# Two-part start of a hybrid diffusion layer: 768 token columns through two projection blocks, then the last 512

## The chip, the cores and the metric

The kernel runs on one core of a Trainium2 chip. The metric is device time in microseconds of one execution of the whole program; lower is better. All names of engines are those of the profile: PE (TensorE matmul), PEld (TensorE weight load), DVE (VectorE), ACT (ScalarE), POOL (GpSimd), SP (SyncE, which issues most DMAs).

## The reference

One layer over 256 context tokens and 1024 latent tokens, model width 1024, everything in float32. What matters here is its beginning:

```python
def rms_norm(x, w):
    y = xf * lax.rsqrt(jnp.mean(xf * xf, axis=-1, keepdims=True) + EPS)
    return y * w
def modulate(h, shift, scale):
    return h * (1 + scale) + shift
```

`shift` and `scale` come from SiLU(c) for latent tokens and SiLU(c_ctx) for context tokens through one linear map `w_ada` (adaLN). So the normed and modulated input is h = x * root * w1s + shift, with one root factor per token (column) and one w1s = (1 + scale) * norm weight and one shift per channel (row), different for context and latent. One input projection of h follows: gated DeltaNet q, k, v, z and gates, and neighbourhood attention q, k, v. Then come short convolutions, two scans, attention, the output projection with a gated residual, and a SwiGLU feed-forward.

## The kernel before, in words

Tokens lie in the free dimension: `xcT[k]` is 128 channels by 1280 tokens (`CT` = 256 context columns first, then 1024 latent), for k = 0..7 (`KT` = 8). `SEGS` cuts the 1280 columns into 256, 512 and 512, one PSUM bank each. PSUM has 8 banks, which `bank(name)` hands out.

Float32 products are made of three products in the faster fp32r form: each operand is split into a high part and a rounding remainder (`hh[k]`, `hl[k]` for h; `whi`, `wlo` for a weight block), and PE adds hi*hi, hi*lo and lo*hi. The remainder needs the high part first: `hh` is written on ACT, `hl` is h minus `hh`.

The beginning, with the lines of the profile:

- SP issues, in this order, the eight x tiles of 1280 columns (L686), two raw weight blocks (`fraw`, L690), `w_ada` tiles 0 to 2 (L682, 1 MB each), constants `cst` and `masks` (L693, L694), `w_ada` tiles 3 to 7, and small tables.
- Squares on ACT (L743, L745), pairs added on DVE (L746), summed over channels by a product with ones on PE (L748, in plain float32, which PE makes in two passes), Ln and Exp on ACT (L750, L751): the root factors `rs`, in SBUF.
- The weight blocks of the first two jobs, `first[0]` and `first[1]` (keys of head 0 and 1), are split on DVE and on POOL (L201, L204).
- `ada(j)` multiplies SiLU(c) with w_ada tile j on PE (L712) and copies the row to SBUF (L714). `column(j)` turns that row into columns on PE (L720) and writes `mod1` (shift) and `w1s` on DVE (L722, L725). `keep_busy` issues products whose result nobody reads (L759).
- `normed_tile(k)`: for each stretch of columns x * w1s * rs on DVE (L732), then hh = that + shift on ACT (L733); then hl = (that + shift) - hh on DVE (L735).
- For k = 0 the products of both blocks are written out by hand (L773); for k = 1..7 `normed_tile(k+1)` is issued ahead of `b.mm([k])` for both blocks (L419: nine products of 256, 512, 512 columns), and `AHEAD` says behind which of them the next `ada` and `column` stand.

In this part (`tc.manual_schedule`) PE, DVE and ACT run in the order in which the code is written. Outside it a planner orders instructions by its own estimates.

Behind the part, each block is evacuated (`evac`: a scaled copy on ACT at L452, four taps of the convolution on DVE at L461, reading the bank in PSUM), and the next jobs follow: `jobs[2]` is another key block, whose weights are split at L203 and L204 and whose high part takes the place of block 0's. Its products need three banks: two are free, one comes from block 0's evacuation.

Of the kernel before, what the change touches and what calls it, by code (L numbers as in the profile page):

```python
# [9 lines left out]
F32 = mybir.dt.float32  # L10
# [4 lines left out]
OP = mybir.AluOpType  # L15
# [5 lines left out]
KT = 8  # L21
# [67 lines left out]
def hybrid(ctx, tc, a, dbg):  # L89
# [83 lines left out]
    act.activation(sc2, c2, AF.Silu)  # L173
# [215 lines left out]
    with ExitStack() as bs:  # L389
# [281 lines left out]
        first = [Block("k", 0), Block("k", 1)]  # L671
        with ExitStack() as xs:
            xp = pools(xs, "xp", "left")
            xt = []
            masks = xp.tile([128, 4, 128], F32, name="masks", tag="masks")
            ascope = ExitStack()
            wap = pools(ascope, "wap", "right", 7)
            aw = {}

            def load_ada(j):  # L680
                aw[j] = w = wap.tile([128, KT, 256], F32, name="wada", tag="wada")
                sp.dma_start(w, a["wa1"][j])  # L682

            for k in range(KT):
                x = xp.tile([128, T], F32, name=f"xt{k}", tag=f"xt{k}")
                sp.dma_start(x, a["xcT"][k])  # L686
                xt.append(x)
            raws = [xp.tile([128, KT, 128], F32, name=f"fraw{i}", tag=f"fraw{i}") for i in range(2)]
# [15 lines left out]
            rs = xp.tile([128, T], F32, name="rs", tag="rs")  # L704
            rows = {}

            def ada(j, copy):
# [6 lines left out]
                copy(rows[j], p[:, :256])  # L714

            def column(j):

                p, row = bank("pm"), rows.pop(j)
                for b in range(2):
                    pe.matmul(p[:, 2 * b:2 * b + 2], row[:, b * 128:(b + 1) * 128], sel, start=True, stop=True)  # L720
                m = mod1.rearrange("p (s b) c -> p s b c", s=2)[:, :, j]
                dve.tensor_tensor(m, p[:, 0:4].rearrange("p (s c) -> p s c", s=2),  # L722
                                  bada[:, 0:16].rearrange("p (s b) -> p s b", s=2)[:, :, j:j + 1].to_broadcast(
                                      [128, 2, 2]), OP.add)
                dve.tensor_scalar(w1s[:, j], m[:, 1], 1.0, n1w[:, j:j + 1], op0=OP.add, op1=OP.mult)  # L725

            def normed_tile(k, cuts=(slice(0, CT), slice(CT, T))):
                t = xt[k]
                parts = [(x, mod1[:, k, int(x.start < CT):int(x.start < CT) + 1]) for x in cuts]
                for x, sh in parts:  # L730
# [7 lines left out]
            with tc.manual_schedule(engines={mybir.EngineType.PE, mybir.EngineType.DVE, mybir.EngineType.Activation}):  # L738
# [29 lines left out]
                for b in first:  # L768
                    b.banks()
# [1071 lines left out]
```

## Time and profile before

| What | Value |
|---|---|
| time, median of 3 runs | 1489.84 us (1489.16 to 1491.1) |
| profiled execution, its time | 1489.21 us |
| its span, first to last instruction | 1487.5 us |
| PE busy | 1451.1 us, 98% of the span |
| DVE, ACT, POOL busy | 995.0, 703.9, 106.7 us |
| mean granted TensorE clock | 0.999 |
| first product of a projection block | 25.43 us |
| first product of the third block | 65.31 us |

How to read a row. In the timeline: start in us, busy us, engine, line, operation, output<-inputs, shape, count of merged instructions, and in brackets the idle time before it and what ended it. In the groups: line, engine, operation, names and shapes, count, then busy us and the mean ns of one, then the idle time of the engine before them. Matmuls are pipelined: the pitch from one start to the next says more than the busy time of one.

### The profile page before, as it was taken

What the parts mean: (1) busy time and instruction counts of PE and PEld (TensorE: products, weight loads), DVE (VectorE), ACT (ScalarE), POOL (GpSimd) and SP (SyncE); (2) the same over time, 40 slices, a digit from 0 to 9 for tenths busy, and PEclk for the clock granted to TensorE, in tenths of its full rate; (3) what the DMA queues carried; (4) which work ended last, traced back from release to release, by engine and by line L of the source; (5) the groups of instructions that cost most, each with busy time, mean ns of one, the idle gap of its engine ahead of it and who ended that gap; (6) DMA issues with size and microseconds to landing.
All of it is one profiled execution on the core that took longest, in us unless ns stands there. A gap on an engine that the chain in (4) does not pass through costs nothing.

```text
span 1487.5 us, 23901 instructions
## 1 busy us (share of the span) xinstructions
PE 1451.1 (98%) x8708; PEld 1219.0 (82%) x8708; DVE 995.0 (67%) x1794; ACT 703.9 (47%) x1388; POOL 106.7 (7%) x208
## 2 busy tenths in 40 slices
PE   6999999999999988999999999999999999999998
PEld 4889898887898877887878888888888888888887
DVE  5783598966653546688966589665555557698652
ACT  5452544556653256667752474333333335355440
POOL 1033000311110001112100000000000000000000
PEclk9999999999999999999999999999999999999999
DMA  9265232987664488998458105333333335888742
GB/s 390 74 214 157 75 86 69 287 245 227 199 202 161 124 286 268 284 282 255 138 183 298 43 15 199 121 106 106 107 106 106 107 100 191 291 325 290 255 135 85
DMA packets 205397, 267.35 MB, mean 180 GB/s; under 512 B 15968, under 2 KB 113760, under 8 KB 204256
## 3 DMA queue, kind: packets, MB, share of 16 engines
q1 hardware_dynamic: 197680, 260.01, 54.2%
q10 hardware_dynamic: 7600, 5.81, 1.2%
q8 instruction: 69, 1.13, 0.3%
q14 instruction: 48, 0.39, 0.1%
HBM read 201.02 MB, written 68.94 MB: 181 GB/s over the span
## 4 chain that ended last, share of the span: by engine, by line
PE 59%; DMA 3%; DVE 2%; ACT 2%; issue 1%; SPq 0%; DVEq 0%; ACTq 0%
PE ps L1415 29%; PE ps L1758 14%; PE ps L1544 3%; PE sc L332 2%; PE sc L322 2%; PE ps L1392 2%; PE sc L309 1%; PE blk L615 1%; PE ps L1566 1%; PE ps L1278 1%; DMA bt<-rpb 1%; DVE bt L313 1%; PE ps L1295 1%; PE ps L1269 1%; PE ps L1259 1%
## 5 line engine op out<-in xcount | busy, mean ns | idle before, releaser
L1476 ACT CAST uhi<-wq 128x512 fp32r<-128x512 f32 x101 | 61.3, 622 | 136.5 <-issue 84.6
L1476 ACT CAST uhi<-ws 128x512 fp32r<-128x512 f32 x91 | 53.9, 621 | 147.7 <-PE ps L1415 93.3
L419 PE MATMUL blk<-hh,whi 128*128 128x512 f32 (+1 forms) x410 | 119.8, 386 | 0.5 <-ACT kk L568 0.5
L419 PE MATMUL blk<-hl,whi 128*128 128x512 f32 (+1 forms) x410 | 113.9, 370 | 0.3 <-DVE hl L735 0.3
L615 PE MATMUL blk<-zw,hh 128*128 128x256 f32 (+1 forms) x576 | 112.5, 289 | 1.0 <-ACT cr L467 1.0
L419 PE MATMUL blk<-hh,wlo 128*128 128x512 f32 (+1 forms) x410 | 112.6, 369 | 0.0
L1477 DVE TENSOR_TENSOR ulo<-wq,uhi 128x512 fp32r<-128x512 f32 x101 | 67.9, 689 | 60.2 <-ACT uhi L1476 33.8
L1415 PE MATMUL ps<-hT,uhi 128*128 128x512 f32 x336 | 103.7, 390 | 0.0
L1415 PE MATMUL ps<-hT,ulo 128*128 128x512 f32 x336 | 103.4, 389 | 0.0
L1415 PE MATMUL ps<-lT,uhi 128*128 128x512 f32 x336 | 103.4, 389 | 0.0
L615 PEld LDWEIGHTS blk<-zw,hh 128*128 128x128 f32 x576 | 90.9, 189 | 4.1 <-ACT cr L467 1.4
L1415 PE MATMUL ps<-hB,uhi 128*128 128x512 f32 x288 | 89.1, 390 | 0.0
L1415 PE MATMUL ps<-lB,uhi 128*128 128x512 f32 x288 | 88.7, 389 | 0.0
L1415 PE MATMUL ps<-hB,ulo 128*128 128x512 f32 x288 | 88.7, 389 | 0.0
L419 PEld LDWEIGHTS blk<-hl,whi 128*128 128x128 f32 x410 | 70.9, 188 | 14.1 <-DVE hl L735 0.8
L419 PEld LDWEIGHTS blk<-hh,wlo 128*128 128x128 f32 x410 | 71.1, 188 | 13.7
L615 PE MATMUL blk<-zw,hl 128*128 128x256 f32 (+1 forms) x288 | 81.8, 284 | 0.0
L419 PEld LDWEIGHTS blk<-hh,whi 128*128 128x128 f32 x410 | 67.3, 189 | 15.4 <-issue 4.0
L1415 PEld LDWEIGHTS ps<-lT,uhi 128*128 128x128 f32 x336 | 63.1, 188 | 13.1
L1415 PEld LDWEIGHTS ps<-hT,ulo 128*128 128x128 f32 x336 | 63.1, 188 | 13.1
L1415 PEld LDWEIGHTS ps<-hT,uhi 128*128 128x128 f32 x336 | 62.9, 188 | 13.0
L313 DVE CUSTOM_DVE_ANT_0 bt<-sc,bt 128x640 f32<-128x640 f32 x64 | 52.4, 821 | 29.9 <-DMA bt<-rpb 10.0
(361 smaller groups left out, 3361.5 us busy)
## 6 DMA issues: line engine op xcount, KB each, us to landing
wq<-w_fo SPq DMA_DIRECT2D x99, 256.0 KB, 4.1
wq<-w_gu SPq DMA_DIRECT2D x88, 256.0 KB, 2.9
wad<-wa SPq DMA_DIRECT2D x64, 256.0 KB, 4.3
bt<-rpb SPq DMA_DIRECT2D x64, 192.0 KB, 4.0
t_d<-g SPq DMA_DIRECT2D x22, 512.0 KB, 3.5
fr<-t_d SPq DMA_DIRECT2D x44, 256.0 KB, 4.7
f_d<-g SPq DMA_DIRECT2D x33, 256.0 KB, 2.1
fr<-f_d SPq DMA_DIRECT2D x33, 256.0 KB, 4.1
```

Source lines behind the costliest of these rows:

```text
L309: s = pe.matmul(sc[:, u * 640 + n0:u * 640 + n1], q, ks[i], start=i == 0, stop=i == 1)
L313: dve.tensor_tensor_reduce(bt, sc[:, u * 640:u * 640 + 640], bt, -1.0, 3.0e38, OP.add, OP.min, m[:, 0:1])
L322: pe.transpose(sc[:, u * 640 + j * 128:u * 640 + (j + 1) * 128], bt[:, j * 128:(j + 1) * 128], ident)
L332: return pe.matmul(sc[u * ND:u * ND + ND, 1280:1408], vv, pts[u][:, j * 128:(j + 1) * 128], start=j == 0, stop=j == 4)
L419: pe.matmul(o, ww[:, k], xx[k][:, s], start=k == 0 and j == 0, stop=k == KT - 1 and j == 2)
L615: pe.matmul(p[:, :c1 - c0], x[k][:, s], ww[:, k, c0:c1], start=k == 0 and j == 0, stop=k == KT - 1 and j == 2)
L1392: pe.matmul(o, w[wi][:, k], parts[xi][k][:, s], start=k == 4 and j == 0, stop=k == 3 and j == 2)
L1415: pe.matmul(o, w[wi][:, k], x[xi][:, k], start=first and k == 0 and j == 0, stop=k == n - 1 and j == 2, skip_group_check=True)
L1476: act.copy(hi, self.raw[key])
L1477: dve.tensor_tensor(lo, self.raw[key], hi.bitcast(F32), OP.subtract)
L1544: pe.matmul(o, w[wi][:, k], parts[xi][k][:, s], start=k == 0 and j == 0, stop=k == KT - 1 and j == 2)
L1758: pe.matmul(o[b], w[wi][:, b], F[xn, p][xi], start=n in (0, 1, 5) and p == 0 and j == 0, stop=p == NFB // 2 - 1 and j == 2, skip_group_che ...
```

## The change

The columns are taken in two parts. `HEAD` is the first 768 columns (256 context and 512 latent), `REST` the last 512. The x tiles are loaded in two pieces (`xh`, `xr`). Squares, root factors and products of the head come first, through both blocks and all eight k; then the same for the rest, whose squares are made during the head. The root factors stay in PSUM banks, where DVE's `scaled` reads them. In the head, and for even k in the rest, DVE only multiplies by the root; ACT applies w1s and shift twice, once into `hh` (rounded) and once in place, and POOL subtracts to give `hl`. For odd k of the rest the old form (DVE, ACT, DVE) is kept. The first two weight blocks are rounded on ACT, their remainders made on POOL. POOL, too, now runs in written order in this part. Fourteen tiny products stand ahead of the sums. In the rest's products, some of b1's are kept back behind b0's last.

The diff, without lines taken out that the section above describes:

```diff
+        HEAD, REST = [slice(0, CT), slice(CT, 768)], slice(768, T)
...
-            wap = pools(ascope, "wap", "right", 7)
+            wap = pools(ascope, "wap", "right", 5)
+            lap = pools(xs, "lap", "left", 3)
...
             for k in range(KT):
+                sp.dma_start(xh[k], a["xcT"][k, :, 0:768])
             for i in range(2):
+                load_ada(i)
                 sp.dma_start(raws[i], a["w_conv"][4 + i])
-            for j in range(3):
+            for j in range(2, 5):
                 load_ada(j)
+            load_rest(0, 1)
+            load_ada(5)
+            load_rest(2)
+            load_ada(6)
+            load_rest(3)
+            load_ada(7)
+            load_rest(4, 5, 6, 7)
             sp.dma_start(cst, a["cst"])
             sp.dma_start(masks, a["masks"])
-            for j in range(3, KT):
-                load_ada(j)
...
+            def scaled(k):
+                for s, q in zip(HEAD, rs):
+                    dve.tensor_tensor(xh[k][:, s], xh[k][:, s], q[:, :s.stop - s.start], OP.mult)
+
+            def shifted(k, x, parts):
+                for s, d in parts:
+                    j = int(d.start < CT)
+                    act.activation(hh[k][:, d], x[:, s], AF.Identity, bias=mod1[:, k, j:j + 1], scale=w1s[:, k, j:j + 1])
+                for s, d in parts:
+                    j = int(d.start < CT)
+                    act.activation(x[:, s], x[:, s], AF.Identity, bias=mod1[:, k, j:j + 1], scale=w1s[:, k, j:j + 1])
+                    pool.tensor_tensor(hl[k][:, d], x[:, s], hh[k][:, d].bitcast(F32), OP.subtract)
+
+            def head(k):
+                shifted(k, xh[k], [(s, s) for s in HEAD])
+
+            def tail(k, q):
+                x = xr[k]
+                if k % 2 == 0:
+                    dve.tensor_tensor(x, x, q, OP.mult)
+                    shifted(k, x, [(slice(0, 512), REST)])
+                    return
+                sh = mod1[:, k, 0:1]
+                dve.scalar_tensor_tensor(x, x, w1s[:, k, 0:1], q, op0=OP.mult, op1=OP.mult)
+                act.activation(hh[k][:, REST], x, AF.Identity, bias=sh)
+                dve.scalar_tensor_tensor(hl[k][:, REST], x, sh, hh[k][:, REST].bitcast(F32), op0=OP.add, op1=OP.subtract)
...
+            def unit(b, j, k, rest=False):
+                w, x = b.w[j == 2], (hh, hl)[j == 1][k]
+                outs = b.outs[2:] if rest else b.outs[:2]
+                for o, s in outs:
+                    pe.matmul(o, w[:, k], x[:, s], start=k == 0 and j == 0, stop=k == KT - 1 and j == 1)
...
+                with tc.issue_after(given.ins):
+                    keep_busy(14)
...
+                ada(0)
+                b0.prefetch(raws[0], pool)
+                keep_busy(2)
+                column(0)
+                scaled(0)
+                head(0)
+                keep_busy(6)
...
+                for k in range(2, KT):
+                    unit(b0, 0, k)
+                    unit(b1, 0, k)
+                    if k + 1 < KT:
+                        column(k + 1)
...
+                        head(k + 1)
                     if k == 3:
+                        qs = [square(i, act) for i in range(2)]
+                        pool.tensor_tensor(qs[0], qs[0], qs[1], OP.add)
+                    elif k in (4, 5):
+                        pool.tensor_tensor(qs[0], qs[0], square(k - 2, act), OP.add)
+                    elif k == 6:
+                        q4, q5 = square(4, dve), square(5, dve)
+                        dve.tensor_tensor(q4, q4, q5, OP.add)
+                        dve.tensor_tensor(qs[0], qs[0], q4, OP.add)
+                        q6, q7 = square(6, act), square(7, act)
+                        dve.tensor_tensor(q6, q6, q7, OP.add)
+                        dve.tensor_tensor(qs[0], qs[0], q6, OP.add)
+                    unit(b0, 2, k)
+                    if k < KT - 1:
+                        unit(b1, 2, k)
+                    unit(b0, 1, k - 1)
+                    if k < KT - 1:
+                        unit(b1, 1, k - 1)
+                    if k + 2 < KT:
+                        scaled(k + 2)
+                        ada(k + 2)
+                rs.clear()
+                unit(b0, 1, KT - 1)
+                total, rest = bank(), bank()
+                pe.matmul(total, M[C_ONE], qs[0], start=True, stop=True)
+                act.activation(rest, total, AF.Ln, bias=b_eps, scale=1.0 / D)
+                act.activation(rest, rest, AF.Exp, scale=-0.5)
+                total = None
+                for j, k in ((2, KT - 1), (1, KT - 2), (1, KT - 1)):
+                    unit(b1, j, k)
...
+                for k in range(KT):
+                    tail(k, rest)
+                rest = None
+                later = []
+                for k in range(KT):
+                    unit(b0, 0, k, True)
+                    unit(b0, 2, k, True)
+                    if k:
+                        unit(b0, 1, k - 1, True)
+                    if k == KT - 1:
+                        unit(b0, 1, k, True)
+                    later += [(0, k), (2, k)] + [(1, k - 1)] * bool(k) + [(1, k)] * (k == KT - 1)
+                    while len(later) > (0 if k < 4 or k == KT - 1 else 3 * k - 9):
+                        j, q = later.pop(0)
+                        unit(b1, j, q, True)
+                act.copy(mr[:, 4], ident)
+                act.copy(mr[:, 0:4], masks)
```

In `unit(b, j, k)` the number j is 0 for hi*hi, 1 for hi times the remainder `hl`, 2 for `wlo` times `hh`.

More of the change, by code (lines that the diff above doesn't have):

```diff
@@ L738, in hybrid @@
[L738 to L745 removed]
+                dve.tensor_scalar(w1s[:, j], p[:, 2:4], bada1[:, j:j + 1], n1w[:, j:j + 1], op0=OP.add, op1=OP.mult)
@@ new lines, in keep_busy @@
+            def keep_busy(n):
+                p = bank("pm")
+                for _ in range(n):
+                    m = pe.matmul(p[:, :128], ones, ones, start=True, stop=True)
+                return m
+            b0, b1 = first
+            with tc.manual_schedule(engines={mybir.EngineType.PE, mybir.EngineType.DVE, mybir.EngineType.Activation,
+                                             mybir.EngineType.Pool}):
+                dve.tensor_scalar(bada1, bada[:, 8:16], 1.0, None, op0=OP.add)
+                with tc.issue_after(given.ins):
+                    keep_busy(14)
+                sums = [bank() for _ in HEAD]
+                for k in range(0, KT, 2):
+                    sq = [xp.tile([128, 768], F32, name="sq%d" % i, tag="sq%d" % i, bufs=2 + i) for i in range(2)]
+                    act.activation(sq[0], xh[k], AF.Square)
+                    if k == 4:
+                        dve.tensor_tensor(sq[1], xh[k + 1], xh[k + 1], OP.mult)
+                    for s in HEAD if k == KT - 2 else [slice(0, 768)]:
+                        if k != 4:
+                            act.activation(sq[1][:, s], xh[k + 1][:, s], AF.Square)
@@ L752, in hybrid @@
-                first[0].prefetch(raws[0], dve, dve)
-                first[1].prefetch(raws[1], pool, pool)
-                w = first[0].w[0]
-                def keep_busy(n):
-                    p = bank("pm")
-                    for _ in range(n):
-                        pe.matmul(p, w[:, 0], w[:, 0:4], start=True, stop=True)
-                ada(0, dve.tensor_copy)
-                keep_busy(3)
+                rs += [bank() for _ in HEAD]
+                for p, q, s in zip(sums, rs, HEAD):
+                    n = s.stop - s.start
+                    act.activation(q[:, :n], p[:, :n], AF.Ln, bias=b_eps, scale=1.0 / D)
@@ L778, in hybrid @@
[L778 to L794 removed]
+                    b.pss = [(bank("blk"), s.start, s.stop - s.start) for s in HEAD]
@@ new lines, in hybrid @@
+                    b.outs = [(p[:, :n], slice(s0, s0 + n)) for p, s0, n in b.pss]
+                unit(b0, 0, 0)
+                scaled(1)
+                ada(1)
+                unit(b0, 2, 0)
+                b1.prefetch(raws[1], pool)
+                column(1)
+                head(1)
+                unit(b1, 0, 0)
+                unit(b0, 1, 0)
+                scaled(2)
+                ada(2)
+                unit(b1, 1, 0)
+                unit(b0, 0, 1)
+                unit(b1, 0, 1)
@@ new lines, in hybrid @@
+                rs.clear()
[7 more added lines that the diff above has]
+                    unit(b1, j, k)
+                for b in first:
+                    b.pss.append((bank("blk"), REST.start, 512))
+                    b.outs.append((b.pss[2][0], REST))
```

99 lines of the change are left out of this document (35 added, 64 removed).

## The prediction

> **What bounds the kernel now.** I read the page first, then busy time by stage, then the waits of PE's weight loads, then the timeline of the first 70 us, and last the groups by shape for durations.
>
> ```profile
> span 1487.5 us, 23901 instructions
> PE 1451.1 (98%) x8708; PEld 1219.0 (82%) x8708; DVE 995.0 (67%) x1794; ACT 703.9 (47%) x1388; POOL 106.7 (7%) x208
> ```
>
> The stages cut at the first product of the first two blocks and behind their last (columns: busy us and count of PE, PEld, DVE, ACT, POOL, then granted clock, DMA share, GB/s), and under them all waits of PE's loads from 65 to 150 us:
>
> ```profile
> 25.40:65.30 39.90, 38.52 (x268) 29.37 (x268) 28.71 (x47) 18.02 (x31) 0.00 (x0) 1.00 0.48 179
> 65.30:150.00 84.70, 83.14 (x559) 75.40 (x558) 54.78 (x115) 34.47 (x71) 24.47 (x36) 1.00 0.56 169
> 150.00:490.00 340.00, 340.00 (x2312) 287.59 (x2312) 236.38 (x321) 176.83 (x323) 36.95 (x86) 1.00 0.56 171
> ```
> ```profile
> PEld blk L633 <- DVE zw L608: 0.9, 1, 0.9
> PEld m L859 <- DVE G L838: 0.9, 1, 0.9
> PEld blk L419 <- ACT kk L568: 0.7, 1, 0.7
> ```
>
> Behind 65.3 us PE is simply full: 2.5 us of waits up to 150, none to speak of up to 490. So a shift of 65.3, the end of the edited part, reaches the end of the kernel nearly whole. The question is when b1's last product is issued. Now:
>
> ```profile
> 25.43 0.28 PE L773 MATMUL blk<-hh,whi 128*128 128x256 f32 x1
> ...
> 61.29 1.29 DVE L735 SCALAR_TENSOR_TENSOR hl<-xt,mod,hh 128x1024 fp32r<-128x1024 f32 x1 [0.83 <-ACT hh L733]
> 62.63 0.30 PEld L419 LDWEIGHTS blk<-hl,whi 128*128 128x128 f32 x2 [0.66 <-DVE hl L735]
> 65.31 0.42 PEld L419 LDWEIGHTS blk<-hh,whi 128*128 128x128 f32 x2
> 65.66 0.42 PEld L419 LDWEIGHTS blk<-hl,whi 128*128 128x128 f32 x2
> ```
>
> First product 25.43, next block at 65.31. DVE keeps the written order: it stands 0.83 us behind ACT although other work exists, and PE waits for it only at the very end (0.66). Remember this pattern, DVE parked behind ACT: the change has it too.
>
> **The change, part by part.** I carry durations of rows along the code's order, engine by engine; done on before from its modulation matmuls on, this gives 65.7 for the 65.31 above, so 0.4 comes off below.
>
> *Start.* Rows for it:
>
> ```profile
> 6.46 1.27 ACT L743 ACTIVATE sq<-xt 128x1280 f32<-128x1280 f32 x1
> 7.63 1.25 ACT L745 ACTIVATE sq<-xt 128x1280 f32<-128x1280 f32 x1
> ```
> ```profile
> 12.34 0.33 PEld L748 LDWEIGHTS m<-sq,ones 128*128 128x128 f32 x1 [0.52 <-issue]
> 13.19 0.33 PEld L748 LDWEIGHTS m<-sq,ones 128*128 128x128 f32 x1 [0.52 <-issue]
> 15.99 0.19 PEld L748 LDWEIGHTS m<-sq,ones 128*128 128x128 f32 x1 [0.24 <-issue]
> 16.42 0.19 PEld L748 LDWEIGHTS m<-sq,ones 128*128 128x128 f32 x1 [0.24 <-issue]
> ```
> ```profile
> L745 ACT ACTIVATE sq<-xt 128x512 f32<-128x512 f32 x2 | 1.1, 614 | 0.0
> L750 ACT ACTIVATE rs<-m,bias 128x512 f32<-128x512 f32 x2 | 1.4, 688 | 0.6 <-PE m L748 0.6
> L750 ACT ACTIVATE rs<-m,bias 128x256 f32<-128x256 f32 x1 | 0.5, 474 | 2.0 <-PE m L748 2.0
> L203 ACT CAST whi<-wraw 128x1024 fp32r<-128x1024 f32 x1 | 1.0, 1047 | 1.7 <-PE blk L419 1.7
> L733 ACT ACTIVATE hh<-xt,mod 128x512 fp32r<-128x512 f32 x2 | 1.4, 722 | 0.2 <-DVE xt L732 0.2
> L733 ACT ACTIVATE hh<-xt,mod 128x256 fp32r<-128x256 f32 x8 | 4.1, 512 | 10.4 <-DVE xt L732 10.4
> ```
>
> Consecutive ACT instructions overlap by 0.1 (6.46 to 7.63 is 1.17 for 1.27). Between 0.61 for 512 and 1.27 for 1280 a square of 768 is about 0.83, pitch 0.73; six of them and one cut in two end at 11.8, DVE's adds at 13.3. PE has 8 sums; a 512 sum is two passes, 0.85 apart early in the trace and 0.43 later, so one of 768 columns takes 1.28 us when quick. Bounds: 14.6 (only the last sum left) and 16.3 (early pace for the first). The 14 tiny products put ahead of them speak for the quick end, a queue of four sums for the late; I take the middle, 15.5. Then ACT: Ln 0.69, Exp 0.47 and 0.69 (PSUM to PSUM, priced like the Ln), b0's cast 1.05, hh 0.51: 3.4, less overlaps, plus about 0.7 of waiting for PE's result and the scaled tile. First product near **19.2**, 6.2 us earlier than now. The casts come off DVE and POOL and lie on ACT, on the path (included); arow's copies move from ACT to DVE, which is idle there.
>
> One place for a page: the Trainium skill, "TensorE: Matmul & The Clock Gate", section "What's actually happening", says that some 3.4 us of busy PE lift the clock from half to full. The 0.85 and 0.43 pitches agree; by that rule the 14 products would bring the sums to 15.0 and my end 0.5 us forward.
>
> *Transfers.* SP issues 32 instead of 24; the order moves w_ada 0 ahead of the block weights, cst and masks behind everything.
>
> ```profile
> GB/s 0 263 401 394 395 416 428 416 422 403 434 422 417 422 417 389 446 412 432 402 417 422 422 334 276 28 133 40 0 0 60 263 0 0 0 0 0 5 0 10
> wada<-wa SPq DMA_DIRECT2D x8, 1024.0 KB, 15.7
> ```
>
> At some 417 GB/s from about 3 us, 8 x 384 KB and w_ada 0 have landed by 13, ahead of 15.5; all eight remaining x tiles by 38, first wanted on ACT at 36 (the first two, landed by 27) and on DVE at 45. So transfers cost nothing; were they 5 us later, w_ada 0 would set the start. The masks' copies (0.9 us of ACT) move behind the stage, under PE's last products.
>
> *Head, 768 columns.* Pitches on PE:
>
> ```profile
> 37.18 0.65 PEld L720 LDWEIGHTS pm<-bias,arow 128*128 128x128 f32 x4
> 37.84 0.59 PEld L712 LDWEIGHTS pm<-wada,wide 128*32 128x32 f32 x16
> 38.84 0.42 PEld L419 LDWEIGHTS blk<-hh,whi 128*128 128x128 f32 x3 [0.41 <-issue]
> ```
> ```profile
> 69.94 0.19 PEld L419 LDWEIGHTS blk<-hh,wlo 128*128 128x128 f32 x1
> 70.17 0.19 PEld L419 LDWEIGHTS blk<-hh,whi 128*128 128x128 f32 x1
> ```
>
> A unit of 256+512 columns is 0.35 (65.31 to 65.66), one of 512 alone 0.23, ada 1.0, column 0.66. Up to b0's last-but-one unit: 44 x 0.35 + 7 x 1.66 = 27.0, plus 1.3 of early waits (second half of the first tile, rows, POOL's first remainders): 47.5. The loop takes 6 x 0.35 + 1.66 = 3.8 us; ACT has four activations, 2.1, and a square; POOL has remainders:
>
> ```profile
> L386 POOL TENSOR_TENSOR na<-no,na x8: 1268/1280/1742, 557.7 to 762.1; 128x512 fp32r<-128x512 f32 x8
> L572 POOL TENSOR_TENSOR kd<-kk,cst 128x1280 f32<-128x1280 f32 x4 | 11.8, 2957 | 93.0 <-ACT kk L568 93.0
> L204 POOL TENSOR_TENSOR wlo<-fraw,whi 128x1024 fp32r<-128x1024 f32 x1 | 3.2, 3244 | 0.1
> L204 DVE TENSOR_TENSOR wlo<-fraw,whi 128x1024 fp32r<-128x1024 f32 x1 | 1.9, 1939 | 0.0
> L204 DVE TENSOR_TENSOR wlo<-wraw,whi 128x1024 fp32r<-128x1024 f32 x1 | 1.2, 1224 | 1.9 <-ACT whi L203 1.9
> L735 DVE SCALAR_TENSOR_TENSOR hl<-xt,mod,hh 128x512 fp32r<-128x512 f32 x2 | 1.4, 748 | 0.0
> L1714 DVE TENSOR_TENSOR e<-ps,e 128x512 f32<-128x512 f32 x20 | 12.9, 686 | 25.2 <-PE ps L1415 25.2
> ```
>
> POOL: 1.28 for 512, by the line through 512 and 1280 0.7 for 256 and 2.4 for 1024; with a square sum 3.3 per loop. Hidden, with 0.5 to spare. But with both at work at once POOL took 3244 for those 2400 and DVE 1939 instead of 1224. DVE's head work reads one operand in PSUM (686 as in L1714); whether that spares it no row says, and I take it as spared.
>
> *End of the head: a chain.* Column 7 ends near 44.4. Behind it w1s and mod 0.5, ACT's four 2.1, POOL 1.3: the last remainder at 48.6, PE waits 1 us. Meanwhile ACT's last squares end at 48.3, DVE's last two adds at 49.8, the sum on PE 0.85, Ln and Exp 1.7 with latencies: root at 52.4; scaling 0.69 and hh 0.72: first product of the last 512 columns at 53.9. To cover it PE has four units (1.4) queued behind the sum; some 4 us are lost.
>
> *Tail, 512 columns.* PE needs 48 x 0.23 = 11.0. But DVE issues, in order: scale even, scale odd, odd remainder (waits for ACT), next even. ACT issues hh even, shift even, hh odd. One turn is 0.69 + 0.72 + 0.70 + 0.72 + 0.75, less 0.2: **3.4 us per pair against 2.76 on PE**. Parked behind the waiting odd remainder is the next pair. Four turns from 52.4: 66.0. Then 15 products (b0's last two, b1's saved 13) 3.4: 69.4.
>
> *Both engines on SBUF at once.* In the tail each odd remainder (two SBUF operands) starts with POOL half through its even one, and around 45 to 50 us DVE's square sums meet POOL's. Bounds: 0, and the stretch of the rows (DVE x1.58, POOL x1.35) on all of it, about 6 us. I take a third, as each overlap is partial: 1 us ahead of the root, 0.3 for each turn, together 2.2. The Trainium skill, "SBUF — State Buffer", section "Who interferes with whom", holds that a DVE instruction with two SBUF inputs contends with a GpSimd instruction that reads SBUF, under an exclusive lock. The 1939 beside 1224 agrees; by a full lock each turn would wait out POOL's remaining 0.6, and the sum would be 1.2 us later.
>
> *Sum.* 69.4 + 2.2 - 0.4 = 71.2 against 65.3: +5.9. In return b0 is finished 3 us before b1 and DVE is free 3 us before PE's end, so its evacuation starts earlier against PE than now; at most the 2.5 us of waits above can go, I take half: 1.2. Net **+4.7 us**. The profiled execution took 1489.21 us (span 1487.5), 0.6 under the median 1489.84; +4.7 on the median is 1494.5.
>
> **The rivals.**
> - *PE paces the tail* (the side that is not slower). If the pair's turn is under 2.76 us, PE runs 11.0 through from 53.9 and ends at 64.9 - 0.4 = 64.5: -0.8, with the 1.2 -2.0, so 1487.8. For it: ACT and DVE each have only 2.1 us of work per pair. Against: the 0.83 row, DVE parked in written order. It decides at 2.76. Chance 0.2.
> - *POOL falls behind in the head.* If DVE's PSUM-reading scalings slow it too, 3.3 x 1.35 = 4.5 per loop exceeds 3.8; five loops with square sums or the last remainder add 3.5, the tail 1: 1499. For: 3244. Against: in the loop DVE has no instruction with two SBUF operands, as L204 had. Chance 0.2.
> - *It does not start earlier*: the casts on ACT, POOL's first lo or w_ada hold PE to about 25. Then the tail costs all of 12: 1500. Chance 0.07.
> - *All waits covered*: from 19.2, 48 x 0.58 + 7 x 1.66 + 0.85 = 40.3, end 59.5, 1484. Chance 0.05.
>
> **How the numbers follow.** My forecast has 0.48, its own range 1491.5 to 1497.5 (contention 0 to 4, start half a us either way). 0.2% is 3 us, about what this measurement tells from no change. Faster: the last rival and a part of the first, 0.13; same: most of the first and the forecast without contention, 0.27; slower 0.60. Range 1487.5 to 1500.
>
> **What would show it.** First product of b0 at 18.7 to 20; products of the head at the 3.8 us loop; a gap on PE of 2 to 4 us after the square sum; odd remainders on DVE idling about 1.4 behind ACT; pairs 3.4 to 3.8 apart; next block at 69 to 73. Wrong if the pairs come at 2.8, if POOL's 512 remainders exceed 1.5 in the head, or if later stages end by other waits than now.

## The result, and the profile after

The changed kernel takes 1501.58 us (median of 5 runs, 1499.86 to 1502.4) where the kernel before takes 1491.10 (5 runs on the same chip, 1489.16 to 1491.65): a ratio of 1.0077, 95% interval 1.0065 to 1.0089. The profiled execution of the changed kernel took 1502.4 us with a span of 1500.6 us. The forecast was +4.7 us, 1494.5, in a range up to 1500; the medians differ by 10.5.

Totals of the page first, then the stages cut where the prediction cut them: at the first product of the first two blocks and behind their last one (columns as there).

```profile
span 1500.6 us, 24032 instructions
...
PE 1464.1 (98%) x8740; PEld 1227.2 (82%) x8740; DVE 991.1 (66%) x1800; ACT 718.8 (48%) x1416; POOL 130.4 (9%) x231
```
```profile
18.25:74.30 56.05, 47.19 (x286) 31.42 (x286) 32.74 (x61) 38.55 (x62) 29.75 (x25) 0.94 0.48 185
74.30:150.00 75.70, 73.08 (x495) 66.60 (x494) 41.77 (x63) 32.55 (x64) 20.42 (x28) 0.98 0.60 180
```

PE is "98% busy" in both kernels and says nothing. The stage says it: 39.9 us before, 56.05 now, for the same block products and some small ones, with PE busy for 47.2 of them and a granted clock of 0.94 where it was 1.00. The stage starts 7.1 us earlier and ends 9.0 later.

The timeline of the changed kernel, from the first product to the third block (lines behind the edited part have moved by 105):

```profile
18.29 0.39 PE L775 MATMUL blk<-hh,whi 128*128 128x256 f32 x1
...
45.85 2.82 POOL L747 TENSOR_TENSOR hl<-xh,hh 128x256 fp32r<-128x256 f32 x2
...
53.07 0.69 DVE L755 TENSOR_TENSOR xr<-xr,m 128x512 f32<-128x512 f32 x1 [2.52 <-ACT m L876]
54.66 0.50 PE L775 MATMUL blk<-hh,whi 128*128 128x512 f32 x1 [1.89 <-ACT hh L743]
...
55.53 1.28 POOL L747 TENSOR_TENSOR hl<-xr,hh 128x512 fp32r<-128x512 f32 x1 [6.86 <-ACT xr L746]
56.10 1.25 DVE L761 SCALAR_TENSOR_TENSOR hl<-xr,mod,hh 128x512 fp32r<-128x512 f32 x1 [1.68 <-ACT hh L760]
57.28 0.68 DVE L755 TENSOR_TENSOR xr<-xr,m 128x512 f32<-128x512 f32 x1
...
59.73 1.30 POOL L747 TENSOR_TENSOR hl<-xr,hh 128x512 fp32r<-128x512 f32 x1 [2.92 <-ACT xr L746]
60.30 1.28 DVE L761 SCALAR_TENSOR_TENSOR hl<-xr,mod,hh 128x512 fp32r<-128x512 f32 x1 [1.69 <-ACT hh L760]
61.50 0.67 DVE L755 TENSOR_TENSOR xr<-xr,m 128x512 f32<-128x512 f32 x1
...
68.71 1.27 DVE L761 SCALAR_TENSOR_TENSOR hl<-xr,mod,hh 128x512 fp32r<-128x512 f32 x1 [1.68 <-ACT hh L760]
...
74.33 0.41 PEld L419 LDWEIGHTS blk<-hh,whi 128*128 128x128 f32 x2
...
76.75 1.21 DVE L204 TENSOR_TENSOR wlo<-wraw,whi 128x1024 fp32r<-128x1024 f32 x1
...
78.01 0.41 PEld L419 LDWEIGHTS blk<-hh,wlo 128*128 128x128 f32 x3 [2.56 <-DVE wlo L204]
```

Read it in three places. In the tail DVE begins a pair at 53.07, 57.28 and 61.50: 4.2 us per turn, and in each turn it stands 1.68 us behind ACT with the next pair's scalings queued behind the wait. The odd remainder takes 1.25 to 1.28, where the same instruction took 0.75 before. Then, 15 products after the last remainder starts, the third block is there at 74.33, 9.02 behind the 65.31 of before; and at once PE waits 2.56 for that block's low weight part, a wait that the kernel before does not have.

The clock by windows of 3.4 us (granted TensorE clock is the number before the DMA share):

```profile
65.80:69.30 3.50, 1.54 (x5) 0.78 (x5) 1.82 (x3) 2.86 (x5) 1.16 (x1) 1.00 0.00 0
69.30:72.70 3.40, 3.40 (x8) 2.44 (x8) 2.98 (x6) 3.37 (x8) 0.13 (x1) 0.50 0.00 0
```

While PE waits in the tail the clock is full; in the window after that, when PE at last has work, it is half. 8 products start in it, where 15 start in the next one (72.7 to 76.1).

How far PE's matching products are behind those of the kernel before, product by product, at times of the kernel before: 9.0 us at the stage's end, 13.0 at 79 us, 12.2 from 101, 15.2 from 298 (a further window pair of half clock there), 13.0 from 590, 13.2 at the end. So two thirds of the loss are made in the edited stage, and instead of the 1.2 us given back that the prediction booked, the next stage adds 3 to 4.

### The profile page after: what moved, and what is told of

It reads as the page before. It is cut to its first block, busy times and chain, and to the rows that moved or that the text cites. A ratio compares the mean times of both kernels' runs of the same rounds, so it can differ in the third digit from the quotient of the medians.

```text
span 1500.6 us, 24032 instructions
## 1 busy us (share of the span) xinstructions
PE 1464.1 (98%) x8740; PEld 1227.2 (82%) x8740; DVE 991.1 (66%) x1800; ACT 718.8 (48%) x1416; POOL 130.4 (9%) x231
## 4 chain that ended last, share of the span: by engine, by line
PE 51%; ACT 1%; DVE 1%; issue 0%; DVEq 0%
PE ps L1520 28%; PE ps L1863 14%; PE ps L1649 3%; PE ps L1497 2%; PE ps L1671 1%; PE sc L322 1%; PE sc L309 1%; PE sc L332 1%; DVE bt L313 0%; ACT sq L1424 0%; PE ps L1374 0%; ACT oacc L1441 0%; PE ps L223 0%; PE ps L1395 0%; PE ps L1400 0%
## 5 line engine op out<-in xcount | busy, mean ns | idle before, releaser
L1581 ACT CAST uhi<-ws 128x512 fp32r<-128x512 f32 x91 | 53.9, 621 | 146.5 <-PE ps L1520 92.3
L419 PE MATMUL blk<-hh,whi 128*128 128x512 f32 (+1 forms) x368 | 109.5, 391 | 0.5 <-ACT kk L568 0.5
L419 PE MATMUL blk<-hh,wlo 128*128 128x512 f32 (+1 forms) x368 | 101.9, 372 | 2.1 <-DVE wlo L204 2.1
L419 PE MATMUL blk<-hl,whi 128*128 128x512 f32 (+1 forms) x368 | 103.6, 374 | 0.0
L419 PEld LDWEIGHTS blk<-hh,wlo 128*128 128x128 f32 x368 | 64.2, 189 | 15.1 <-DVE wlo L204 2.6
L419 PEld LDWEIGHTS blk<-hl,whi 128*128 128x128 f32 x368 | 64.4, 190 | 12.3
L1520 PEld LDWEIGHTS ps<-lT,uhi 128*128 128x128 f32 x336 | 63.1, 188 | 13.2
L419 PEld LDWEIGHTS blk<-hh,whi 128*128 128x128 f32 x368 | 61.0, 191 | 12.9 <-issue 2.4
```

What stands on the lines that cost most here:

```text
L419: pe.matmul(o, ww[:, k], xx[k][:, s], start=k == 0 and j == 0, stop=k == KT - 1 and j == 2)
L1520: pe.matmul(o, w[wi][:, k], x[xi][:, k], start=first and k == 0 and j == 0, stop=k == n - 1 and j == 2, skip_group_check=True)
L1581: act.copy(hi, self.raw[key])
```

## Experiments

Theory A, formed on the two traces: the tail's turn sets the end of the stage (the next pair parked behind the odd remainder, and the remainder itself stretched by GpSimd), and two additions come on top: half clock on PE after poorly filled windows, and the third block's split, now queued on DVE behind the convolution. Rivals: PE or the root sets the end anyway; the clock falls where PE waits in any case and costs nothing; the split's wait is repaid later.

**e1_unpark: the odd remainder is issued behind the next pair's scalings.**

```diff
                 act.activation(hh[k][:, REST], x, AF.Identity, bias=sh)
-                dve.scalar_tensor_tensor(hl[k][:, REST], x, sh, hh[k][:, REST].bitcast(F32), ...)
+            def odd(k):
+                dve.scalar_tensor_tensor(hl[k][:, REST], xr[k], mod1[:, k, 0:1], hh[k][:, REST].bitcast(F32), ...)
...
                 for k in range(KT):
                     tail(k, rest)
+                    if k % 2 and k > 1:
+                        odd(k - 2)
+                odd(KT - 1)
```

> Edit: in the tail the odd remainder of a pair is issued on DVE behind the next pair's two scalings instead of ahead of them; nothing else. Theory (DVE parked behind ACT, with remainders of 1.27 us beside POOL, makes the turn of 4.2 us): the turn falls to what PE needs, 12 products of 0.23 = 2.8, or to DVE's own 0.68 + 0.73 + 1.27 = 2.7; from the first product of the last 512 columns (54.7) to the next block 11 to 12.5 us instead of 19.7; the kernel 7 us faster than the changed one, about 1494. Rival (POOL's even remainder behind ACT's second activation sets the pace): turn stays above 3.8, gain under 1.5 us.

Measured: 1495.79 us (1494.26 to 1498.19), ratio to before 1.0038 [1.0023, 1.0052], 5.8 below the changed kernel. (This run and the next three ran on another chip than the result, where the kernel before had 1490.74; e5 to e7 on one where it had 1489.32, e8 and e9 on one where it had 1489.29. Ratios, each against the kernel before on the same chip, compare across these groups better than medians.)

```profile
59.11 0.68 DVE L755 TENSOR_TENSOR xr<-xr,m 128x512 f32<-128x512 f32 x1
...
59.52 1.29 POOL L747 TENSOR_TENSOR hl<-xr,hh 128x512 fp32r<-128x512 f32 x1 [0.88 <-ACT xr L746]
60.37 0.99 DVE L763 SCALAR_TENSOR_TENSOR hl<-xr,mod,hh 128x512 fp32r<-128x512 f32 x1
61.28 0.67 DVE L755 TENSOR_TENSOR xr<-xr,m 128x512 f32<-128x512 f32 x1
...
69.05 0.41 PEld L419 LDWEIGHTS blk<-hh,whi 128*128 128x128 f32 x2
...
73.74 0.56 PEld L419 LDWEIGHTS blk<-hh,wlo 128*128 128x128 f32 x3 [3.57 <-DVE wlo L204]
```

A pair in the middle of the tail now takes 2.2 us (59.11 to 61.28) without a wait on DVE, and the third block comes 5.3 us earlier, although in this execution the tail's first scaling is 1.8 later (54.89) and PE has half clock from 50.1 to 60.3. The parked pair is the largest single cause. But the split still stands behind eleven taps, and PE waits 3.57 for it: of the 5.3 us, 4.2 are left behind that wait (8.8 behind the kernel before, where the changed kernel is 13.0). Note the remainder: it starts inside GpSimd's instruction, which ends at 59.52 + 1.29 = 60.81, and itself ends at 61.36.

**e2_clock: products that nobody reads ahead of PE's waits** (4, 5 and 9 of 128 columns around the root, 2 or 4 for each k of the tail).

```diff
+                keep_busy(4)
                 unit(b0, 1, KT - 1)
+                keep_busy(5)
...
+                    if k:
+                        keep_busy(4 if k % 2 == 0 else 2)
                     unit(b0, 0, k, True)
```

> Edit: products that nobody reads (128x128 in float32, about 0.21 us each) are put on PE ahead of its waits: 4 and 5 around the last head product, 9 ahead of the first of the last 512 columns, 2 or 4 ahead of each later k. Theory (after a stretch of 3.4 us in which PE was busy for a third or less, PE runs the next 3.4 us at half clock, pitch 0.43 instead of 0.23): no half-clock stretch is left between 45 and 80 us, b1's last 13 products take 3.0 instead of 4.9 us, the next block starts 1.5 us earlier, about 1500. The turns of the tail stay at 4.2. Rival (half clock falls only where PE waits anyway): next block within 0.4 us of 74.3, or later by the added products.

Measured: 1499.10 (1497.9 to 1501.15), 1.0060 [1.0045, 1.0075]: 2.5 below the changed kernel, whose interval (1.0065 to 1.0089) this one overlaps.

```profile
65.80:69.30 3.50, 2.85 (x18) 2.22 (x16) 1.82 (x4) 2.70 (x5) 1.00 (x1) 1.00 0.00 0
69.30:72.70 3.40, 3.35 (x14) 2.29 (x13) 2.97 (x6) 3.37 (x8) 0.28 (x1) 1.00 0.00 0
```
```profile
73.26 0.41 PEld L419 LDWEIGHTS blk<-hh,whi 128*128 128x128 f32 x2
...
78.18 0.65 PEld L419 LDWEIGHTS blk<-hh,wlo 128*128 128x128 f32 x3 [3.80 <-DVE wlo L204]
```

Useless work took the half windows out of the stage: full clock in the window in which the changed kernel had 0.50. The third block comes 1.07 earlier, less than the 1.5 expected. But what PE won, it then waited: 3.80 for the split, which DVE begins at 76.91 here and at 76.75 in the changed kernel, and this wait earns a half window at 78.3 after all. Behind it the execution is 13.2 behind the kernel before, no better than the 13.0 of the changed kernel. So half clock moves the stage's end, and this run does not show that it costs the program any time; the 2.5 us of the medians have no place in the trace.

**e3_split: the third block's split ahead of block 0's evacuation.**

```diff
-        first[0].evac()
         jobs[2].prefetch()
+        first[0].evac()
```

> Edit: the third block's weights are split ahead of block 0's evacuation in the code; nothing in the first two blocks changes. Theory (behind the edited part PE waits 2.5 us for the third block's low weights because DVE does eleven taps of block 0 first): the wait goes, the shift against the kernel before is 9 us at 79 us instead of 13, the kernel 2.5 to 4 us faster than the changed one, 1498. Rival (DVE is simply short of time here): the wait comes back at the next evacuation or the next split, gain under 1 us.

Measured: 1499.83 (1498.56 to 1500.76), 1.0062 [1.0047, 1.0077]: 1.75 below, and not told apart from the changed kernel by its time alone.

```profile
72.89 1.23 DVE L204 TENSOR_TENSOR wlo<-wraw,whi 128x1024 fp32r<-128x1024 f32 x1 [1.97 <-ACT whi L203]
74.03 6.38 DVE L461 SCALAR_TENSOR_TENSOR cacc<-blk,cw,cacc 128x254 f32<-128x254 f32 x12
75.16 0.41 PEld L419 LDWEIGHTS blk<-hh,whi 128*128 128x128 f32 x2
75.50 0.42 PEld L419 LDWEIGHTS blk<-hl,whi 128*128 128x128 f32 x2
75.85 0.43 PEld L419 LDWEIGHTS blk<-hh,wlo 128*128 128x128 f32 x2
```

The split stands ahead of the taps again and PE's wait is gone (75.50 to 75.85). The stage itself ended 0.8 later than in the changed kernel's profile, with half clock from 66.6 to 73.4; what stays is 9.9 us behind at 79 us instead of 13.0.

**e4_three: all three together.**

> Edit: the three edits together. Theory: the next block starts near 66 us, no wait of 2.5 us behind it, no half clock: 10 to 12 us faster than the changed kernel, 1490 to 1492, level with the one before. Rival (the loss sits in the head or in transfers): under 5 us.

Measured: 1492.53 (1491.74 to 1497.05), 1.0019 [1.0010, 1.0028]: 9.0 of the 10.5 us are gone.

```profile
59.22 1.09 PEld L782 LDWEIGHTS pm<-ones 128*128 128x128 f32 x8
60.23 0.19 PEld L777 LDWEIGHTS blk<-hh,whi 128*128 128x128 f32 x1
...
72.00 0.53 PEld L419 LDWEIGHTS blk<-hh,whi 128*128 128x128 f32 x3
```

Yet its third block, 72.00, is later than in e1. Once the pair is not parked, PE has no time to give away, and the unread products, 1.0 us for each four (59.22 to 60.23), stand in front of real ones.

**e5_gap, e6_root and e7_dve:** e1 and e3 with unread products only ahead of the tail; e1 and e3 with the root made earlier and five unread products; and the changed kernel with no work for GpSimd in the tail.

```diff
 e6: squares of tiles 3 and 7 on DVE, 4 to 6 in ACT's gaps; PE adds three partial sums
+                        pe.matmul(total, M[C_ONE], qs[0], start=True, stop=False)
+                        dve.tensor_tensor(q3, q3, q4, OP.add)
+                        dve.tensor_tensor(q5, q5, q7, OP.add)
+                        dve.tensor_tensor(q5, q5, q6, OP.add)
+                        pe.matmul(total, M[C_ONE], q3, start=False, stop=False)
...
+                pe.matmul(total, M[C_ONE], q5, start=False, stop=True)
...
 e7: even remainder on DVE, right ahead of the odd one
-                    shifted(k, x, [(slice(0, 512), REST)])
+                    act.activation(hh[k][:, REST], x, AF.Identity, bias=mod1[:, k, 0:1], scale=w1s[:, k, 0:1])
+                    act.activation(x, x, AF.Identity, bias=mod1[:, k, 0:1], scale=w1s[:, k, 0:1])
...
+                dve.tensor_tensor(hl[k - 1][:, REST], xr[k - 1], hh[k - 1][:, REST].bitcast(F32), OP.subtract)
```

> The odd remainder out of the way, the split ahead of the evacuation, and unread products only ahead of the tail's first product (none inside the tail). If PE paces the tail once nothing is parked on DVE, then the three-fold kernel paid 5.3 us for the unread products inside its tail (0.65, 1.01, 0.56, 1.01, 0.56, 1.01 and 0.57 between its weight loads), and here PE runs 48 products of 0.23 us without a gap, 11.0 us from 55.5-56.2: the third block's first load at 67 (72.0 there, 65.31 before the change), and the run about 4.5 us below 1492.5, at 1488 (1486.5 to 1489.5). If the remainders still pace the tail (odd ones of 1.0 to 1.27 us), the third block is at 70.5 or later and the run at 1491 or above. If the clock falls to half again without the unread products in the tail, one such window costs 1 to 1.5 us: 68.5 and 1489.5.

Measured: 1492.65 (1488.97 to 1495.02), 1.0020 [1.0011, 1.0030]; third block at 67.77, as theory A has it (67), but the time did not follow (1488 was expected). The profiled execution is 1.7 behind the kernel before at 250 us and 5.8 at the end; in between it has half windows at 288.1, 530.4 and 574.8 us. It is, with 1495.02, the slowest of ten, so it doesn't say where the median loses its time.

> The changed kernel with the even remainders of the last columns made by DVE (a subtraction of two SBUF tiles, ahead of the odd remainder) and none by GpSimd; the odd remainder stays where it was, in front of the next pair's scalings. If it is GpSimd's work at the same time that stretches DVE's remainders, all of them take 0.7 to 0.75 us here (odd ones 1.25 to 1.28 in the changed kernel); a pair then takes 0.6 + 0.66 for the scalings, ACT's three operations until 3.0, and remainders until 3.75: turns of 3.75 instead of 4.2, the third block about 1.8 us earlier than 74.33, and the run at 1499.5. If the odd remainder is long for another reason (its operands, the tiles' places), it stays at 1.25, the turn is 4.25 and the run is at 1501.5 or above.

Measured: 1501.56 (two runs, 1501.24 and 1501.89), 1.0086 [1.0067, 1.0104].

```profile
56.81 0.69 DVE L762 TENSOR_TENSOR hl<-xr,hh 128x512 fp32r<-128x512 f32 x1 [1.07 <-ACT xr L757]
57.43 0.75 DVE L763 SCALAR_TENSOR_TENSOR hl<-xr,mod,hh 128x512 fp32r<-128x512 f32 x1
58.09 0.68 DVE L755 TENSOR_TENSOR xr<-xr,m 128x512 f32<-128x512 f32 x1
...
61.79 0.68 DVE L755 TENSOR_TENSOR xr<-xr,m 128x512 f32<-128x512 f32 x1
...
73.54 0.41 PEld L419 LDWEIGHTS blk<-hh,whi 128*128 128x128 f32 x2
```

With GpSimd at rest the odd remainder is back at 0.75, and the turn is 3.70 (58.09 to 61.79) though DVE makes both remainders. So the stretch from 0.75 to 1.25 comes from GpSimd's work, and without it the parked turn would have been the 3.7 that the prediction had for it with contention. The time was a miss: 1499.5 was expected. In this execution the tail's first scaling stood 1.3 later than in the changed kernel (54.39, half clock from 50.7), b1's products fell into the half window 67.8 to 71.2, and PE waited 3.16 for the third block's split, where most of the 0.8 us went that the stage had won (73.54 against 74.33).

> As the run beside it, but the root of the last 512 columns is made ahead of the end of the head: the squares of tiles 4 to 7 go into gaps of ACT and DVE as soon as the tiles have landed (by 40.8 us), PE adds three partial sums, and ACT's logarithm and exponential follow the last head tile at once, at about 47.7. No unread products but five ahead of the tail. If the late root (52.4 in the changed kernel) is what the rest of the gap comes from, the first product of the last columns starts at 50.5 (54.66 in the changed kernel), PE's 11 us follow without a wait, the third block is at 62.5 (65.31 before the change) and the run at 1484 (1482.5 to 1486): faster than before the change by 0.4%. If the squares beside GpSimd's subtractions stretch both (0.69 to 1.1-1.8, 1.28 to 1.74), the last head remainder ends at 50 or later, the first product at 52, the third block at 64 and the run is at 1486. If time won in this stage isn't kept behind it, the third block is at 62.5 and the run still at 1487 to 1488.

Measured: 1490.41 (1488.34 to 1492.05), 1.0006 [0.9994, 1.0017]: not told apart from before. Of the 4 us expected over e5, 2.2 came by the medians.

```profile
46.69 0.77 PEld L777 LDWEIGHTS blk<-hl,whi 128*128 128x128 f32 x4
...
49.47 0.42 PEld L883 LDWEIGHTS m<-sqb,ones 128*128 128x128 f32 x2
...
52.06 0.69 DVE L755 TENSOR_TENSOR xr<-xr,m 128x512 f32<-128x512 f32 x1 [5.46 <-ACT m L885]
...
66.01 0.41 PEld L419 LDWEIGHTS blk<-hh,whi 128*128 128x128 f32 x2
```

The sum's last operand was ready at 46.6 (DVE's last addition, 45.91 and 0.69), but I had put its product behind eight units in PE's order: it starts at 49.47, and DVE stands 5.46 us for the root. A chain that is shortened on three engines and left at its old place on the fourth stays long.

**e8_root2: e6 with the last two products of the sum ahead of tile 7's units, no unread products; and e9_two: e1 and e3 together, without a single unread product.**

```diff
+                    if k == 6:
+                        pe.matmul(total, M[C_ONE], q3, start=False, stop=False)
+                        pe.matmul(total, M[C_ONE], q5, start=False, stop=True)
+                        act.activation(rest, total, AF.Ln, bias=b_eps, scale=1.0 / D)
+                        act.activation(rest, rest, AF.Exp, scale=-0.5)
...
```

> As the kernel with the early root, with PE's order mended: there the third product of the sum stood behind eight units of head work and started at 49.47, though its operand was ready at 46.6, and the root was ready at 52.0. Here both last products of the sum stand ahead of tile 7's units, the logarithm and the exponential follow the head's last activations at 47.7, and no unread product is left; three of the second block's head units fill PE's first wait in the tail. If the root's place in PE's order is what was left, the first product of the last columns starts at 50.5 (53.65 there, 54.66 in the changed kernel), PE then has 12.1 us of products, the third block is at 63 (66.01 there, 65.31 before the change), and the run 3 us below 1490.4, at 1487.5: 0.1% to 0.2% faster than before the change. If the tail is then paced by ACT, DVE and GpSimd (2.2 to 2.45 us per pair, the last remainder 9.8 us behind the root, then 15 products of 0.23), the third block is at 64 and the run at 1488.5. If PE's clock falls without unread products, one half-clock window adds 1 to 1.5 us.

Measured: 1490.38 (1488.74 to 1493.41), 1.0009 [1.0000, 1.0018]. The stage does about what was expected (51.27 and 63.64, for 50.5 and 63), and the time does not follow:

```profile
51.27 0.19 PEld L777 LDWEIGHTS blk<-hh,whi 128*128 128x128 f32 x1 [1.51 <-ACT hh L743]
...
63.64 0.41 PEld L419 LDWEIGHTS blk<-hh,whi 128*128 128x128 f32 x2
...
94.05 1.28 DVE L608 TENSOR_TENSOR zw<-wraw,zw 128x1088 fp32r<-128x1088 f32 x1
...
100.28 0.09 PEld L633 LDWEIGHTS blk<-hh,zw 128*16 128x16 f32 x1 [1.71 <-ACT zw L607]
...
102.24 0.13 PEld L633 LDWEIGHTS blk<-hh,zw 128*16 128x16 f32 x2 [1.84 <-DVE zw L608]
```
```profile
98.80:102.20 3.40, 0.41 (x2) 0.11 (x2) 1.97 (x3) 3.06 (x6) 0.00 (x0) 0.96 1.03 306
102.20:105.60 3.40, 3.36 (x17) 2.32 (x18) 3.33 (x7) 0.31 (x2) 2.96 (x2) 0.54 0.91 255
```

The third block is 1.67 us earlier than before the change. Then PE runs into the z weights. Their second half shares one raw buffer with the first; SP can issue its transfer only when DVE's split of the first half is done (94.05 + 1.28, issued at 95.36, landed at 99.11). Then DVE splits it only at 100.90, behind an addition (L238) that had waited for a `w_ada` transfer until 100.23. Before the change the same two steps are at:

```profile
91.55 1.28 DVE L608 TENSOR_TENSOR zw<-wraw,zw 128x1088 fp32r<-128x1088 f32 x1
...
101.22 0.11 PEld L633 LDWEIGHTS blk<-hh,zw 128*16 128x16 f32 x2 [0.92 <-DVE zw L608]
```

PE waits there before the change too, but for 0.92. Matching products are 1.6 us ahead at 79 us, 1.0 behind when PE gets its weights, and, with the half window that follows 3.4 us of near idleness, 2.5 behind; 2.1 of these come back at transfers near 575 us. In e6 the same place takes the shift from +0.7 to -0.06. So in these executions the z weights, which hang on DVE's order from 91 to 101 us, decide what is left of the stage's gain. This is read from the traces: no run with a second raw buffer or another order there was made, so it is not shown by experiment.

> The changed kernel with the odd remainder out of the way and the split ahead of the evacuation, and without a single unread product: what is left against the kernel that also had them ahead of the tail (third block at 67.8, 1492.65) is PE's clock alone. If windows of half clock cost time here, one or two of them fall between 48 and 66 us, products of the tail are 0.42 us apart in them, the third block is at 69 to 69.5 and the run at 1494 (1493 to 1495.5). If the clock costs nothing (PE waits for the others in any case), the third block is at 67.8 and the run at 1492.6 or below, since no unread product stands in PE's order.

Measured: 1492.84 (1488.8 to 1494.25), 1.0016 [1.0005, 1.0027]; third block at 67.38, half clock in one window of the stage, 55.6 to 59.0.

Here the rival is right: against e5 (67.77, 1492.65), taking all unread products out costs nothing. Once the turn is shorter than PE's own work, the windows in the tail are full by themselves, and the one half window left comes behind the window in which PE waits for the root's chain. Parking and split alone thus bring the ratio from 1.0077 to 1.0016, and unread products add nothing to that (1.0019 in e4, 1.0020 in e5).

**e10_again and e12_third: the changed kernel unchanged, two more profiles; e11_before: the kernel before, a second one.**

> The changed kernel once more, for a second profiled execution of the same instructions. If the windows of half clock (3.41 us long) lie on a grid that runs on by itself, and a window follows one in which PE was busy for a third or less, then the grid's phase differs here: the half windows fall elsewhere within the stage (55.6, 69.3 and 79.5 us in the first profile), the third block's start moves by up to 1.5 us from 74.33, and the half window at 298 us (3.1 us lost there) can be missing. If the clock follows the work and not a grid, the windows are at 55.6, 69.3, 79.5 and 298.0 again, within 0.5 us of the stage's own shift. The tail's turns are 4.2 us in both cases, the third block's first split stands behind eleven taps of the convolution, and the wait for it is 2 to 3.5 us.

> The kernel before once more, for a second profiled execution. If half clock comes from windows in which PE is busy for a third or less, and this kernel has none behind 14 us whatever the grid's phase (lowest share 0.52), there is no half window between 17 and 250 us here either, and the third block starts at 65.3 within 0.2. Half windows near 290 or 530 us may appear, where the other kernels had them. If half windows in the first 80 us appear here too, they are no property of the change.

> The changed kernel a third time: as the second. Over the three profiles the tail's turns stay at 4.2 us within 0.1 where no odd cause enters, and only what the half windows lie on differs: the third block between 73 and 75.5, the shift at 101 us between 10.5 and 13.5, the end between 9 and 13.5 us behind the kernel before.

Measured: 1499.98 and 1500.54 us, and 1489.13 for the kernel before. In the second and third profiles of the changed kernel the turns are 4.2 again and DVE takes eleven taps ahead of the split; the half windows are elsewhere, 50.2 to 60.5, 67.3 to 74.1 and 81.0 in the one, 52.0 to 58.8, 69.0 and 79.3 in the other, and none is near 298. Of the second profile:

```profile
77.50:80.90 3.40, 1.24 (x6) 1.10 (x7) 3.40 (x6) 0.56 (x1) 0.00 (x0) 1.00 0.00 0
80.90:84.40 3.50, 3.50 (x12) 2.89 (x11) 3.50 (x8) 2.85 (x3) 0.00 (x0) 0.51 0.56 167
```
```profile
75.90 0.42 PEld L419 LDWEIGHTS blk<-hh,whi 128*128 128x128 f32 x2
...
79.66 0.42 PEld L419 LDWEIGHTS blk<-hh,wlo 128*128 128x128 f32 x3 [2.64 <-DVE wlo L204]
```

The third block is at 75.90 (0.4 outside what was expected) and 74.58, the wait for the split 2.64 and 2.95, the shift at 101 us 13.8 (0.3 outside) and 12.9, at the end 10.8 and 11.3. So the loss in the stage and the wait behind it are the kernel's; the loss at 298 us is chance. The kernel before has no half window from 17 to 250 us in either profile (the second has one at 527.7), and its stage is not fixed to 0.2 us as I had thought: in the second profile x tiles landed later (ACT waited 1.9 for them, 1.2 in the first), and its third block was at 66.28. That 0.98 was gone at the end, where it was 0.1 ahead of the first.

## Why the prediction was right and wrong

*The start, the transfers and the head held.* First product 18.29 (19.2 forecast; 18.99 and 18.78 in the other profiles): ACT's logarithm of the last sum starts at 14.71, so the sums ended by the quick bound, 14.6, and not by the middle, 15.5. Loop 3.74 (3.8), GpSimd's pair of head remainders 1.99 (0.7 + 1.28), transfers hidden. "POOL falls behind in the head" and "it does not start earlier" are out, and so is "all waits covered", by the wait at 54.66. DVE's scalings with one operand in PSUM do not slow GpSimd, as taken: its 512-column remainder took 1.28 to 1.29 with them beside it.

*The end of the head held in sum.* First product of the last 512 columns 54.66, forecast 53.9 plus 1 of contention. (The terms for the last head remainder, 44.4 + 0.5 + 2.1 + 1.3, add up to 48.3, not to the 48.6 written; PE takes it at 48.73.) The contention is there: GpSimd's pair of remainders takes 2.82 at 45.85 instead of 1.99. The close fit owes something to luck: in the other two profiles half clock meets the product of the square sum (from 50.2 and 52.0), and the same product starts at 56.30 and 55.29.

*The step that failed first is the turn.* Forecast 3.4 and 0.3 of contention, measured 4.2, four times: 1.8 us on the end of the last remainder (69.98 against 52.4 + 1 + 4 x 3.7 = 68.2). e7 parts it: 3.7 without GpSimd, so 0.3 is ACT's longer operations (0.81 with a scale per partition where I had put 0.72, and the gaps between engines), and 0.5 is the stretch. The Trainium skill, "SBUF — State Buffer", section "Who interferes with whom", calls the port pair that DVE and GpSimd share an exclusive lock, and says that issue order decides who blocks. The rows agree that the second comer waits for the end of the first: the odd remainders end 0.54 to 0.55 us behind the end of GpSimd's instruction, whether they started 0.57 (the changed kernel) or 0.85 (e1) after its start. They do not show a block from the first moment: alone the remainder takes 0.75, so about 0.2 of it is not held up. The forecast had named this lock, with 0.6 for each turn, and taken a third as a partial overlap, 0.3; the 0.5 measured is nearer to the lock.

*The mechanism was right.* "Parked behind the waiting odd remainder is the next pair", and 2.76 as the point from which PE paces the tail: e1 takes the parking away and the turn falls to 2.2; in e8 PE then goes through 12.1 us of products in 12.4 (51.27 to 63.64). The rival that PE paces the tail was thus wrong for this kernel and right for e5, e8 and e9.

*The step that was missing is PE's clock.* The 15 products behind the last turn were priced at the full clock, 3.4, less the correction 0.4; 74.33 - 69.98 = 4.35. That is the other 1.35 of the 3.1 us by which the stage's end (71.2 forecast) was missed; about 1.2 of it are six products 0.43 apart, from 70.19 on, instead of 0.23. It explains the stage's end only: in e2 nothing of it was left behind the wait for the split. I had quoted half-speed rows from the start of the trace and not asked whether a tail that PE spends half idle would bring them back.

*The step that had the wrong sign is what follows.* I booked 1.2 us as given back because DVE is free earlier. It is free, and uses the time for eleven taps of block 0 (70.32 to 76.8) ahead of the third block's split: PE waits 2.56 (e3 removes it), and that wait earns another half window at 79.5. Together +4.0 at 79 us, of which 0.8 returns at 101 us, since PE has a wait of 0.92 for the z weights there before the change, and, in all three profiles, 1.6 to 2.8 near 575 us. The order of the planner's part is an outcome of the change too; I took it as given, though "if later stages end by other waits than now" stood among the signs of being wrong, and that sign came. The premise that a shift of 65.3 "reaches the end of the kernel nearly whole" fails for gains as well: of the 1.67 us that e8 wins in the stage, none is left at the end, where its profile is 0.4 behind.

*The sum.* Profile against profile +13.2: +9.0 in the stage (forecast +5.9), +3.2 more by 101 us (forecast -1.2), +3.1 at 298 by chance, -2.1 behind. By medians +10.5; the other two profiles, without the chance at 298, end at +10.8 and +11.3. Shown to cost time are the parking (ratio 1.0038 without it) and, in its trace, the split; both together give 1.0016 (e9). The clock's own price on the run is not shown: e2's time is not told apart from the changed kernel's, and e9 does as well as e4 and e5 without any unread product. No version here is measurably faster than the kernel before: e6 and e8, which end the stage 0.7 behind and 1.7 ahead of it, are at 1.0006 and 1.0009.

## What to carry over

When an engine waits in written order, price what is queued behind the wait, and price two-operand SBUF work on DVE that starts beside a GpSimd instruction as held until that one ends (here 0.5 us more for 0.75), not as a part of an overlap. When PE becomes the waiting engine, price the work that follows at the lower clock as well, and then look whether the next wait swallows it. And a stage that ends earlier is worth only what the next wait leaves: look for the next transfer whose issue hangs on another engine's order before counting the gain.

## What the runs showed of the hardware that was not expected

- *Half clock without an idle stretch.* The granted clock changes in windows of 3.41 us on a grid that differs between executions of the same kernel (the first half window inside the stage at 55.6, 50.2 and 52.0). In the three profiles of the changed kernel, from 14 to 110 us, all eight windows at full clock in which PE was busy for 0.91 to 1.75 us came ahead of half ones; of five with 1.97 to 2.21 one did; fuller ones never. Half windows with 1.92 to 2.40 us of busy PE were followed by another, those with 3.09 or more by full clock. This is a count, not a rule: near 578 us of the third profile a window with 1.6 stayed full. The longest wait of PE's loads in these places was 2.95 us. The Trainium skill, "TensorE: Matmul & The Clock Gate", section "HAM oscillation — how this bites in real kernels", gives as its rule no idle gaps of PE over about 3.4 us; by that rule alone none of these windows would have been half, and the measurement decides. That the window runs freely, as that page has it in section "What's actually happening", agrees: the grid lies elsewhere in each profile.
- *The second comer waits.* A DVE remainder of 128x512 with two SBUF operands: 0.75 alone (e7), 1.25 to 1.28 started 0.57 us into a GpSimd subtraction of 1.28, 0.99 started 0.85 into it (e1); always done 0.54 to 0.55 after it. GpSimd's instruction took 1.28 to 1.30 in all of these.
- *ACT.* 128x512 with bias and scale per partition took 0.81, with the bias alone 0.71. The Trainium skill, "ScalarE: Activation LUTs", section "What ACT_TABLE_LOAD costs", adds some 93 ns for each operand that is read per partition; the trace agrees (0.10).
